# A 96-byte tile at the end of the right side of SBUF in a hybrid pooling, linear-attention and MLP block

## The chip, the cores and the metric

One core of one Trainium2 chip. The metric is the device time of one execution in microseconds (us); smaller is better. A core has TensorE (matmuls, PE in the profile; its weight loads are PEld), VectorE (DVE), ScalarE (ACT), GpSimd (POOL), and SyncE (SP), which here issues the DMA transfers. SBUF, the on-chip memory, has 128 partitions; a tile takes the same bytes in each of them, so an address below is a byte within a partition.

## The reference

One block over 16 meta tokens and 1,024 tokens of width 1,024, all in float32:

```python
h = concat([meta, x])
u = rmsnorm(h, norm_mix)
a, q, k, v, r, lr, ga, gb = split(u @ w_in)          # 512, 256, 256, 512, 512, 16, 1024, 1024 columns
p = (trailing means of a over 2, 4, 8, 16 positions, less a, mixed per group) * pool_scale
y_a = p @ w_pool_out
log_a = log_sigmoid(lr @ w_gate_up + b_gate) / 16
o = gla_chunked(q / 8, k, v, log_a)                  # 4 heads, chunks of 64, a state carried across
y_b = (rmsnorm(o) * silu(r)) @ w_gla_out
h = h + (sigmoid(ga) * y_a + sigmoid(gb) * y_b) @ w_out
h = h + square(relu(rmsnorm(h, norm_ffn) @ w_ff1)) @ w_ff2    # d_ff = 4096
return rmsnorm(h, norm_final)[16:]
```

## The kernel before

**Numbers in two parts.** A float32 operand is split into `hi` (rounded to the type fp32r) and `lo` (the rest): ScalarE copies, VectorE subtracts (in `split`, L607 and L608; in the weight ring, L75 and L76). A product is then three matmuls, hi x hi, hi x lo, lo x hi (`mm3`, L258, L259, L260). In a call `mm3(ps, n, lhs, rhs)` the `lhs` is the stationary operand, which is loaded into TensorE's array, and the `rhs` is the moving one, which streams through it. "Product" below means one accumulated run of four such triples, 12 matmuls, mostly of 128x512.

**Stages, in their order.**
1. `start` (L389): eight row tiles of x are normed and transposed into `th0`/`tl0` (tokens 0 to 511 behind the 16 meta tokens) and `th1`/`tl1` (tokens 512 to 1023). Beside that `v_tile` (L348) multiplies each row tile (stationary) with the two column halves of the v weights, `vw0` (272 columns, with those of lr) and `vw1` (256): nine tiles each, one of them for the meta tokens.
2. Blocks of a and k (`a_block`, `k_block`, through `project`, L265), each as two pieces of 264 columns and one of 512, all streamed from `th`/`tl`, and the pooling.
3. `pairs_of_projections` (L686): q, r, gb and ga, two column blocks at a time with seven products instead of eight (P1 to P7, Strassen's scheme). P1 and P2 stream `th0` behind the meta tokens, P5 and P3 `th1`, P6, P7 and P4 the difference tiles `t0`, `t1`, `t2`. The inner part of the linear attention runs beside it.
4. `gla` (L1105): the state across chunks, with `ya_block` and `yb_block` as filler. `yb_block` (L1002) streams `yg`; its second half of the tokens runs on into the next stage.
5. `out_tile` (L1177): for each of eight row tiles the product with `w_out`, first the columns 0 to 511 from `wo0`, then 512 to 1023 from `wo1`, with `MH`/`ML`, views of `th`/`tl`, as stationary operands. Each is 24 matmuls, two products.
6. `ff1` (L1304): 16 turns (NPAIR) of seven products, in the order P6, P1, P7, P5, P4, P2, P3. P4 streams `t4h`/`t4l`, P6 and P7 `wo0`'s memory, the others `th`/`tl`. The results go to DRAM (`hf_dram`).
7. `ff2` (L1433): seven sums m = 0 to 6 over 16 steps i, each step one product of 12 matmuls (four row tiles times three). Both operands are split into slots that are dealt out in turn (`next_slot`, L598): four in `w1h`/`w1l` and three in `fxh`/`fxl`. Beside m = 0 the blocks of `w_ff2` are loaded.

The order on TensorE is the order of the program text; the other engines' is made by the scheduler from the program. All DMA transfers are issued by SP in one queue.

**Memory.** Two stacks of tiles grow towards each other (`Stack`, L35; L116): `left` from low addresses, `right` from the end of SBUF downwards. A tile is pushed when a stage needs it and popped when a later stage opens. On the right stand, over the run, `xr`, `vw0`, `vw1`, `vo`; then `rawp0`, `rawp1`, `fs`, `s3`, `u2p`, `u3p` and the tiles of the inner linear attention (`n`, `f`, `ends`, `g`, `gi`); then `yg1`, `yg0`, `o`, `gi`, `v`, `sr`, `on`, `kt`, `w`; then `u2p`, `rawx0`, `wo1`; then `fs`, `s3`, `u3p`, `t4h`, `t4l`, `rawx1`; then `bt`, `fxh`, `fxl`. Each has a size per partition that is a multiple of 128 bytes. On the left stand `raw0`, `raw1` (load buffers), `w1h`, `w1l`, `th0`, `tl0`, `th1`, `tl1`, `t0` to `t2`, `wo0`, `acc`, `h`, the four `w2` tiles, `c` and others.

In the kernel before, the right side ends at byte 229,344, which is 1,791 x 128 + 96. As every size there is a multiple of 128, every tile on the right begins 96 bytes past a multiple of 128 (`t4h` at 202,720 = 1,583 x 128 + 96). From `raw0` (23,424 = 183 x 128) on, the working tiles of the left begin at multiples of 128 (`th1` at 81,792 = 639 x 128). Within a tile, rows mostly are multiples of 512 bytes. Two exceptions: a row of `th0` has 528 columns, 2,112 bytes, so its rows begin at 0 and 64 bytes past a multiple of 128 by turns, and the tokens behind the 16 meta tokens begin another 64 bytes on; and a row of `vw0` has 272 columns, 1,088 bytes.

Of the kernel before, what the change touches and what calls it, by code (L numbers as in the profile page):

```python
# [7 lines left out]
F32 = mybir.dt.float32  # L8
# [6 lines left out]
P = 128  # L15
# [88 lines left out]
def kernel(  # L104
# [9 lines left out]

    act, dve, pool, pe = nc.scalar, nc.vector, nc.gpsimd, nc.tensor
    left, right = Stack(tc, "left"), Stack(tc, "right")  # L116

    psp, ps_open = {}, []

# [1375 lines left out]
    banks()  # L1495
    left.pop_to(0)
    right.pop_to(0)


# [33 lines left out]
```

## Time and profile before

| | |
|---|---|
| median of 3 runs | 1259.6 us (1257.75 to 1259.92) |
| the profiled execution | 1261.11 us, span 1259.2 us, mean granted clock of TensorE 0.994 |
| busy in the span | PE 1223.6 us, PEld 998.9, DVE 865.8, ACT 634.6, POOL 74.1 |
| DMA | 192.23 MB, 153 GB/s over the span |

The span runs from the first to the last instruction of the program; the execution's own time lies 1.9 us above it. A busy share is an average over stages with different limits. Matmuls overlap: one of 128x512 is shown with some 390 to 400 ns, and the next one starts 220 to 240 ns behind it. So the pace of TensorE is read from the starts in its timeline, not from the durations. A row of the timeline gives the start, the duration, the engine, the source line, the operation, out<-in by the program's tile names without their last numbers (`th0` and `th1` are both `th`, `wo0` and `wo1` both `wo`; a name that stands for both operands appears once), the shapes, and, where the engine sat idle before, for how long and what ended that.

### The profile page before, as it was taken

The numbers are of one execution on the slowest core, as the hardware profiler recorded it, in microseconds if no ns is written. First come the engines' busy times: TensorE is split into PE (matmuls) and PEld (weight loads), VectorE is DVE, ScalarE is ACT, GpSimd is POOL, SyncE is SP. The second block draws the span as 40 slices with busy tenths as digits, with TensorE's granted clock in tenths as the row PEclk, the third lists the DMA queues.
The fourth block names the chain that finished last, engine by engine and source line by source line (L and its number), as shares of the span: only waits on it lengthen the run. The fifth ranks groups of instructions, "written<-read, shape, count | busy, mean of one in ns | idle before, by whom it ended". The sixth has DMA issues, their size and how long they took to land.

```text
span 1259.2 us, 18413 instructions
## 1 busy us (share of the span) xinstructions
PE 1223.6 (97%) x6807; PEld 998.9 (79%) x6807; DVE 865.8 (69%) x1421; ACT 634.6 (50%) x1119; POOL 74.1 (6%) x95
## 2 busy tenths in 40 slices
PE   8999999999999999999999999999999999999997
PEld 6999877777777777788778888888878788888776
DVE  5635549686787478834896676676664886887685
ACT  6623456676666334523664455454453444445444
POOL 0000052332220000000000000000000000000000
PEclk9999999999999999999999999999999999999999
DMA  8312353334337975931245454444479763332532
GB/s 241 95 39 85 94 133 83 120 101 134 92 128 244 322 248 183 332 117 51 100 134 160 134 167 144 149 152 151 157 251 379 258 203 104 94 96 89 168 92 83
DMA packets 153401, 192.23 MB, mean 153 GB/s; under 512 B 12096, under 2 KB 89168, under 8 KB 153312
## 3 DMA queue, kind: packets, MB, share of 16 engines
q1 hardware_dynamic: 153312, 191.06, 47.3%
q8 instruction: 53, 0.87, 0.3%
q14 instruction: 36, 0.29, 0.1%
HBM read 129.14 MB, written 61.88 MB: 152 GB/s over the span
## 4 chain that ended last, share of the span: by engine, by line
PE 72%; DMA 10%; DVE 9%; ACT 5%; issue 3%; SPq 1%; POOL 0%; DVEq 0%; ACTq 0%; POOLq 0%
PE b_o L259 7%; PE b_o L260 7%; PE b_o L258 7%; PE b_mm L258 6%; PE b_mm L260 6%; PE b_mm L259 5%; PE b_y L258 5%; PE b_y L260 5%; PE b_y L259 5%; PE b_z L258 3%; PE b_z L259 3%; PE b_sc L258 3%; PE b_z L260 3%; PE b_sc L259 3%; PE b_sc L260 3%
## 5 line engine op out<-in xcount | busy, mean ns | idle before, releaser
L607 ACT ACTIVATE w1h<-raw 128x512 fp32r<-128x512 f32 x106 | 66.0, 624 | 57.8 <-PE b_sc L259 19.5
L258 PE MATMUL b_sc<-th,w1h 128*128 128x512 f32 x216 | 86.2, 399 | 2.4 <-ACT u2p L718 1.8
L258 PE MATMUL b_z<-th,w1h 128*128 128x512 f32 x216 | 85.6, 396 | 0.7 <-DVE c L726 0.7
L259 PE MATMUL b_z<-tl,w1h 128*128 128x512 f32 x216 | 85.0, 393 | 0.4 <-DVE tl L1219 0.4
L259 PE MATMUL b_sc<-tl,w1h 128*128 128x512 f32 x216 | 85.1, 394 | 0.0
L260 PE MATMUL b_z<-th,w1l 128*128 128x512 f32 x216 | 84.8, 393 | 0.0
L608 DVE TENSOR_TENSOR w1l<-raw,w1h 128x512 fp32r<-128x512 f32 x106 | 72.8, 687 | 17.1 <-ACT w1h L607 17.1
L260 PE MATMUL b_sc<-th,w1l 128*128 128x512 f32 x216 | 84.4, 391 | 0.0
L607 ACT ACTIVATE w1h<-fs 128x512 fp32r<-128x512 f32 x81 | 50.9, 628 | 54.5 <-PE b_y L259 30.2
L258 PE MATMUL b_o<-w1h 128*128 128x512 f32 x192 | 75.5, 393 | 2.7 <-DVE h L1359 1.7
L259 PE MATMUL b_o<-w1l,w1h 128*128 128x512 f32 x192 | 75.9, 395 | 1.2 <-DVE w1l L608 1.2
L260 PE MATMUL b_o<-w1h,w1l 128*128 128x512 f32 x192 | 76.0, 396 | 0.1
L258 PE MATMUL b_mm<-th,w1h 128*128 128x512 f32 (+1 forms) x208 | 72.3, 348 | 0.9 <-DVE c L734 0.9
L608 DVE TENSOR_TENSOR w1l<-fs,w1h 128x512 fp32r<-128x512 f32 x81 | 56.9, 703 | 23.0 <-ACT w1h L607 22.9
L259 PE MATMUL b_mm<-tl,w1h 128*128 128x512 f32 (+1 forms) x208 | 71.1, 342 | 0.0
L260 PE MATMUL b_mm<-th,w1l 128*128 128x512 f32 (+1 forms) x208 | 71.0, 342 | 0.0
L607 ACT ACTIVATE w1h<-bt 128x512 fp32r<-128x512 f32 x45 | 28.3, 630 | 57.7 <-issue 33.9
L1407 DVE TENSOR_TENSOR bt<-w,w 128x512 f32<-128x512 f32 x80 | 54.7, 683 | 2.3 <-DMA w<-in_w_ff_dram 2.3
L258 PEld LDWEIGHTS b_sc<-th,w1h 128*128 128x128 f32 x216 | 40.5, 188 | 13.7 <-ACT u2p L718 2.2
L259 PE MATMUL b_o<-fxl,fxh 128*128 128x512 f32 x128 | 50.2, 392 | 0.6 <-DVE small L217 0.6
L258 PE MATMUL b_mm<-wo,th 128*128 128x512 f32 x128 | 50.6, 395 | 0.0
L260 PE MATMUL b_o<-fxh,fxl 128*128 128x512 f32 x128 | 50.4, 393 | 0.0
(375 smaller groups left out, 3353.8 us busy)
## 6 DMA issues: line engine op xcount, KB each, us to landing
hf_dram<-h SPq DMA_DIRECT2D x112, 256.0 KB, 2.1
raw<-hf_dram SPq DMA_DIRECT2D x112, 256.0 KB, 2.7
w<-in_w_ff_dram SPq DMA_DIRECT2D x64, 256.0 KB, 4.8
raw<-in_w_in_dram SPq DMA_DIRECT2D x22, 512.0 KB, 4.6
raw<-in_w_ff_dram SPq DMA_DIRECT2D x16, 512.0 KB, 4.4
rawx<-in_w_ff_dram SPq DMA_DIRECT2D x16, 512.0 KB, 4.5
rawp<-in_w_in_dram SPq DMA_DIRECT2D x10, 512.0 KB, 4.9
xs<-in_x_dram SPq DMA_DIRECT2D x8, 512.0 KB, 5.7
```

The source lines that it names most:

```text
L258: pe.matmul(ps, ah, bh, start=first and i == 0, stop=False, skip_group_check=more)
L259: pe.matmul(ps, ah, bl, start=False, stop=False, skip_group_check=more)
L260: pe.matmul(ps, al, bh, start=False, stop=last and i == n - 1, skip_group_check=more)
L607: act.activation(hi, a, ACT.Copy)
L608: dve.tensor_tensor(lo, a, f32(hi), ALU.subtract)
L1407: dve.tensor_tensor(bt, w, S["w2"][q[3:]][:, i], ALU.add if q[2] == "+" else ALU.subtract)
```

## The change

A third stack on the right side gets a single tile, `pad`, of 24 float32 values (96 bytes) in each partition, before anything else is pushed there, and gives it up at the end. No instruction writes or reads it. It lies at bytes 229,248 to 229,343, so every tile on the right begins 96 bytes lower, at a multiple of 128 (229,248 = 1,791 x 128; `t4h` at 202,624 = 1,583 x 128). The tiles on the left stay where they are.

```diff
     left, right = Stack(tc, "left"), Stack(tc, "right")
+    edge = Stack(tc, "right")
+    edge.push("pad", [P, 24], F32)
...
     left.pop_to(0)
     right.pop_to(0)
+    edge.pop_to(0)
```

## The prediction

> **What bounds the kernel now.** I read the page first, its span and the chain of work that ended last.
>
> ```profile
> span 1259.2 us, 18413 instructions
> ...
> PE 72%; DMA 10%; DVE 9%; ACT 5%; issue 3%; SPq 1%; POOL 0%; DVEq 0%; ACTq 0%; POOLq 0%
> ```
>
> TensorE carries 72% of the chain. So a change that makes other engines or transfers quicker is worth little, and one that alters the pace of matmuls is worth what it alters, wherever nothing else is waited for. The change moves the address of every tile on the right side of SBUF and nothing else: no instruction is added, removed or reordered by it. The question is therefore whether TensorE, VectorE, ScalarE or a transfer does the same work at another pace when a tile begins 96 bytes past a multiple of 128 (right side now) instead of on one (left side now, right side after).
>
> The trace of before can answer that, since the same instruction runs on tiles of both sides. I went to the timeline of TensorE, to stretches without idle time, and took the start of the first matmul of each product. A product is four calls of three matmuls, 12 in all, each 128x512, so the distance between two such starts is 12 matmuls. First FF1:
>
> ```profile
> 703.59 0.40 PE L258 MATMUL b_y<-t4h,w1h 128*128 128x512 f32 x1
> ...
> 706.40 0.40 PE L258 MATMUL b_sc<-th,w1h 128*128 128x512 f32 x1
> ...
> 709.16 0.39 PE L258 MATMUL b_z<-th,w1h 128*128 128x512 f32 x1
> ...
> 711.88 0.39 PE L258 MATMUL b_y<-wo,w1h 128*128 128x512 f32 x1
> ...
> 722.76 0.40 PE L258 MATMUL b_y<-t4h,w1h 128*128 128x512 f32 x1
> ```
>
> In "b_y<-t4h,w1h" the first name behind the arrow is the operand that streams through (moving), the second the one that is loaded into the array (stationary). The product from `th1`, a left tile, takes 711.88 - 709.16 = 2.72 us, 226.7 ns a matmul. I call this the floor. The product from `t4h`/`t4l`, the only ones here on the right, takes 706.40 - 703.59 = 2.81, and the one after it, again from a left tile, still 2.76. The whole turn of seven products takes 722.76 - 703.59 = 19.17 where seven floors are 7 x 2.72 = 19.04: 0.13 us too much in every turn, all of it at and just behind the right tile.
>
> Is it the side, or the remainder of the address? The left side has misaligned reads too. In the pairs of projections P1 and P2 stream `th0` from its 17th column on, 64 bytes into rows of 2,112 bytes (16.5 x 128):
>
> ```profile
> 175.36 0.39 PE L258 MATMUL b_y<-t2h,w1h 128*128 128x512 f32 x1
> ...
> 178.08 0.40 PE L258 MATMUL b_sc<-th,w1h 128*128 128x512 f32 x1
> ...
> 180.88 0.40 PE L258 MATMUL b_z<-th,w1h 128*128 128x512 f32 x1
> ```
>
> Both operands of both products are left tiles. The aligned one (`t2h`) takes 2.72, the one at 64 bytes 2.80. So the remainder matters, not the side. FF2 shows it more finely, because its seven operand slots (four of `w1h`/`w1l` on the left, three of `fxh`/`fxl` on the right) are dealt out in turn:
>
> ```profile
> 1000.03 0.40 PE L258 MATMUL b_o<-fxh,w1h 128*128 128x512 f32 x1
> ...
> 1002.84 0.40 PE L258 MATMUL b_o<-fxh 128*128 128x512 f32 x1
> ...
> 1005.59 0.39 PE L258 MATMUL b_o<-w1h 128*128 128x512 f32 x1
> ...
> 1008.35 0.39 PE L258 MATMUL b_o<-w1h 128*128 128x512 f32 x1
> ...
> 1011.08 0.40 PE L258 MATMUL b_o<-fxh 128*128 128x512 f32 x1
> ...
> 1013.84 0.40 PE L258 MATMUL b_o<-w1h,fxh 128*128 128x512 f32 x1
> ...
> 1016.64 0.39 PE L258 MATMUL b_o<-w1h 128*128 128x512 f32 x1
> ...
> 1019.39 0.40 PE L258 MATMUL b_o<-fxh,w1h 128*128 128x512 f32 x1
> ```
>
> One operand from each side costs 2.81 (first product) and 2.80 (sixth), whichever of the two moves; both from the right cost 2.75 and 2.76, both from the left 2.76, 2.73 and 2.75, with the rest of the excess at the changes between them. It looks as if the two reads of TensorE disturb each other when their remainders differ. Whether it is that or the misaligned read alone, after the change both read tiles on multiples of 128, like the floor's. The turn is 1019.39 - 1000.03 = 19.36, against 19.04: 0.32 us too much.
>
> **The change, part by part.** The pad itself holds 96 bytes from start to end and is never written or read. It costs space alone. The sizes of all tiles pushed on the right are multiples of 128 bytes, so all of them move together. Terms:
>
> FF1: 16 turns (NPAIR) of 0.13, 2.1 us. TensorE is what it waits for, so all of it counts.
>
> FF2: 112 products are 16 turns. The first 16 products (m = 0) lie beside their loads:
>
> ```profile
> 935.00:978.00 43.00, 41.31 (x170) 32.82 (x170) 20.59 (x33) 16.60 (x28) 0.00 (x0) 0.96 0.98 357
> 978.00:1165.00 187.00, 186.93 (x812) 152.09 (x812) 147.80 (x247) 81.89 (x147) 0.00 (x0) 1.00 0.45 140
> ```
>
> The columns are the stretch, its length, the busy time of PE, PEld, DVE, ACT and POOL, granted clock, DMA share and GB/s. The DMA engines are 98% busy there, and what they load lies on the left, so I put nothing down for it (bounds 0 and 16/7 x 0.32 = 0.7). In the other 96 products PE never pauses: 96/7 x 0.32 = 4.4 us.
>
> Output projection, second half of the columns (`wo1` on the right; the first half has `wo0` on the left):
>
> ```profile
> 569.81 0.39 PE L258 MATMUL b_mm<-wo,th 128*128 128x512 f32 x1
> ...
> 572.53 0.40 PE L258 MATMUL b_mm<-wo,th 128*128 128x512 f32 x1
> ...
> 575.35 0.39 PE L258 MATMUL b_mm<-wo,th 128*128 128x512 f32 x1
> ```
>
> The last product from `wo0` takes 2.72, the first from `wo1` 2.82. Eight tiles of two halves are 16 products, up to 0.10 each, 1.6; with the 0.08 of the next rows 1.3, and some of it lies beside waits for the norm, so I take 1.2 (bounds 0 and 1.6).
>
> The yb products stream `yg`, on the right:
>
> ```profile
> 498.71 0.48 PE L258 MATMUL b_mm<-yg,w1h 128*128 128x512 f32 x1 [0.78 <-DVE c L1023]
> ...
> 504.40 0.40 PE L258 MATMUL b_mm<-yg,w1h 128*128 128x512 f32 x1
> ...
> 507.20 0.40 PE L258 MATMUL b_mm<-yg,w1h 128*128 128x512 f32 x1
> ...
> 527.91 0.51 PE L258 MATMUL b_mm<-yg,w1h 128*128 128x512 f32 x1 [0.80 <-ACT w1h L75]
> ```
>
> 507.20 - 504.40 = 2.80, 0.08 over the floor; 16 products (four blocks, two halves, two outputs) make 1.3. But this stage pauses for VectorE and for a weight block that ScalarE splits, and those come no sooner when PE is early. I take about half, 0.7 (bounds 0 and 1.3).
>
> The v tiles of the start stream `vw`, on the right, against `th`:
>
> ```profile
> 67.99 0.28 PE L258 MATMUL b_mm<-vw,th 128*128 128x256 f32 x1
> ...
> 70.87 0.28 PE L258 MATMUL b_mm<-vw,th 128*128 128x256 f32 x1
> ...
> 117.30 0.28 PE L258 MATMUL b_mm<-th,w1h 128*128 128x264 f32 x1
> ...
> 120.20 0.29 PE L258 MATMUL b_mm<-th,w1h 128*128 128x264 f32 x1
> ```
>
> Twenty-four matmuls of 256 columns take 2.88; at the floor's pace by column they would take 24 x 256/512 x 0.2267 = 2.72. The 0.16 can go wholly in the four tiles where `vw1` meets the aligned `th1`: 0.64. In the others one side stays at 64 bytes in every other row (`th0`, and `vw0` with rows of 1,088 bytes). What is left there I take from the second pair: 264 columns of `th0`, at 0 and 64 by turns, take 2.90 for 24 against 2.81 by the floor, 0.09. So the four tiles of `vw1` with `th0` gain some 0.07 each, 0.3, and those of `vw0` next to nothing. Together 0.9 (bounds 0, and 18 x 0.16 = 2.9).
>
> Other engines, edits with one answer:
>
> ```profile
> L608 DVE TENSOR_TENSOR w1l<-raw,w1h 128x512 fp32r<-128x512 f32 x106 | 72.8, 687 | 17.1 <-ACT w1h L607 17.1
> L607 ACT ACTIVATE w1h<-raw 128x512 fp32r<-128x512 f32 x106 | 66.0, 624 | 57.8 <-PE b_sc L259 19.5 <-PE b_y L259 17.8 <-issue 6.0
> ...
> L608 DVE TENSOR_TENSOR fxl<-raw,fxh 128x512 fp32r<-128x512 f32 x48 | 32.8, 684 | 0.6 <-ACT fxh L607 0.6
> ...
> L607 ACT ACTIVATE fxh<-raw 128x512 fp32r<-128x512 f32 x48 | 29.8, 620 | 13.3 <-PE b_o L260 6.1 <-DMA raw<-hf_dram 3.4 <-issue 3.1
> ```
>
> The split of a left tile into `w1` (all left) takes 687 and 624 ns, into `fx` (right) 684 and 620. The misaligned side isn't slower, so alignment gives these engines nothing. A load of the same 512 KB to the left and to the right:
>
> ```profile
> raw<-in_w_ff_dram SPq DMA_DIRECT2D x16, 512.0 KB, 4.4
> rawx<-in_w_ff_dram SPq DMA_DIRECT2D x16, 512.0 KB, 4.5
> ```
>
> At most 0.1 us a load, asked for a turn ahead: nothing, and if the cover were gone, the 0.1.
>
> Sum: 2.1 + 4.4 + 1.2 + 0.7 + 0.9 = 9.3 us. The profiled execution took 1261.1, 1.5 above the median of the runs, with a span of 1259.2. I take the gain off both: 1251.8 for a profiled execution, 1259.6 - 9.3 = 1250.3 for the median. What is next late in FF2 is VectorE, 147.80 of 187 us busy: 79%, and 80% at the floor's pace, so it can follow.
>
> **A rule that speaks against it.** The Trainium skill, "SBUF — State Buffer", in its note on SBUF cachelines, makes 16 bytes the unit that a read is charged by. Since 96 is six such lines, by that rule a contiguous read is the same before and after, and the time stays 1259.6. "TensorE: Matmul & The Clock Gate" (Part 2, the fill step) says that throughput is purely the N columns fed in, and gives the two operands independent read ports; by that too nothing changes. The trace disagrees: the same 12 x 512 columns take 2.72 or 2.81, and 64 bytes, four lines, are enough.
>
> **Rivals.** *No effect*, 1259.6: the slow products would stem from something that goes with the right tiles (their distance, the slots), or the pad might be rounded to a size that leaves the remainder. For it: I see remainders only through the tiles that have them. Against it: the slow left product at 178.08. 6%.
>
> *PE gains and waits instead*, at the largest term. If VectorE's bursts at the ends of m in FF2 set the pace, the 4.4 are lost: 9.3 - 4.4 = 4.9, 1254.7. Against it: the 80% above. 10%.
>
> *All of it lands*, also where I put waits: 2.1 + 16 x 0.32 + 1.6 + 1.3 + 2.9 = 13.0, 1246.6. Against it: the loads of m = 0, and the 64-byte rows. 6%.
>
> *Slower*: a quicker PE catches up with its feeders, pauses longer, and the clock drops.
>
> ```profile
> 935.68 0.47 PE L258 MATMUL b_o<-w1h 128*128 128x512 f32 x1 [1.72 <-DVE h L1359]
> ...
> 937.01 0.63 PE L260 MATMUL b_o<-w1h,w1l 128*128 128x512 f32 x1
> ...
> 940.41 0.39 PE L259 MATMUL b_o<-fxl,w1h 128*128 128x512 f32 x1
> ```
>
> Behind a pause of 1.72 us eight matmuls take 940.41 - 937.01 = 3.40 instead of 1.81, 1.6 us lost (0.96 granted in that stretch). Its place would be FF2, where each m ends in a burst on VectorE. It decides from (9.3 + 2.5)/1.6, eight such pauses more; then 1259.6 - 9.3 + 8 x 1.6 = 1263.1. Against it: before has one in FF2, and the denser stretch behind it has clock 1.00. 3%.
>
> **How the numbers follow.** The forecast, gains of 6 to 12 us, has 75%. Faster by over 0.2% (2.5 us, about what a measurement of this kernel tells from no change): 75 + 10 + 6 = 91, less 1 for a part-loss that falls inside 2.5: 90%. Within 0.2%: 6 + 1 = 7%. Slower: 3%. The range goes from 1246.5, all of it landing, to 1255.0, where FF2's term is lost; outside lie no effect, slower, and part of the waits.
>
> **What would show it.** In the timeline, products of `t4h`, `wo` (second half) and `yg` at 2.72; the turn of FF1 at 19.04 and of FF2 at 19.04; P1 of the pairs still 2.80, and 264 columns of `th` still 2.90, since they lie on the left. Splits still some 685 and 622 ns. I am wrong if the FF2 turn stays near 19.36, or if it falls and the span doesn't.

## The result, and the profile after

Six runs of the changed kernel took 1252.2 us in the median (1249.28 to 1255.1), six of the kernel before 1259.19. The ratio is 0.9947, 95% interval 0.9929 to 0.9964: 0.5% faster, 7.0 us, where 9.3 were forecast. A second series gave 1249.99 against 1257.7, ratio 0.995 (0.9931 to 0.9969); one run of the kernel before in it, 1346.9 us at a granted clock of 0.849, is left out as slow. The profiled execution of after took 1249.28 us with a span of 1247.4 and a granted clock of 0.996.

The same lines of the page, after (the three instructions more are semaphore instructions of SyncE and ScalarE, which the prediction had not counted on):

```profile
span 1247.4 us, 18416 instructions
...
PE 76%; DVE 9%; DMA 8%; ACT 4%; issue 3%; SPq 1%; POOL 0%; DVEq 0%; ACTq 0%; POOLq 0%
```

In the timeline of TensorE after (the two added source lines move `mm3` from L258 to L260), the first matmul of each product, in FF1 and then one turn of FF2:

```profile
698.01 0.39 PE L260 MATMUL b_y<-t4h,w1h 128*128 128x512 f32 x1
...
700.73 0.39 PE L260 MATMUL b_sc<-th,w1h 128*128 128x512 f32 x1
...
703.45 0.39 PE L260 MATMUL b_z<-th,w1h 128*128 128x512 f32 x1
...
717.05 0.39 PE L260 MATMUL b_y<-t4h,w1h 128*128 128x512 f32 x1
```

```profile
992.03 0.39 PE L260 MATMUL b_o<-fxh,w1h 128*128 128x512 f32 x1
...
1011.07 0.39 PE L260 MATMUL b_o<-fxh,w1h 128*128 128x512 f32 x1
```

The product of `t4h` takes 2.72 us where it took 2.81, the one behind it 2.72 instead of 2.76, and both turns 19.04 instead of 19.17 and 19.36. These rows are typical: of the 15 products of `t4h` without a pause all take 2.81 before, and after all but the first (2.76) take 2.72. The output projection from `wo1`, the yb products, the v tiles and P1 of the pairs:

```profile
568.11 0.39 PE L260 MATMUL b_mm<-wo,th 128*128 128x512 f32 x1
...
570.83 0.39 PE L260 MATMUL b_mm<-wo,th 128*128 128x512 f32 x1
```

```profile
499.55 0.39 PE L260 MATMUL b_mm<-yg,w1h 128*128 128x512 f32 x1
...
502.27 0.39 PE L260 MATMUL b_mm<-yg,w1h 128*128 128x512 f32 x1
...
512.52 0.50 PE L260 MATMUL b_mm<-yg,w1h 128*128 128x512 f32 x1 [1.14 <-ACT w1h L75]
```

```profile
66.61 0.28 PE L260 MATMUL b_mm<-vw,th 128*128 128x256 f32 x1
...
69.49 0.28 PE L260 MATMUL b_mm<-vw,th 128*128 128x256 f32 x1
```

```profile
178.28 0.40 PE L260 MATMUL b_sc<-th,w1h 128*128 128x512 f32 x1
...
181.08 0.40 PE L260 MATMUL b_z<-th,w1h 128*128 128x512 f32 x1
```

`wo1` went from 2.82 to 2.72 and `yg` from 2.80 to 2.72. P1 stays at 2.80, as forecast: both its operands lie on the left. The v tile does not move: 2.88 before, 2.88 after. The 264-column pieces stay at some 2.90 as well, as forecast.

The two profiles differ by 11.8 us of span, more than the medians do. The starts of the same instructions show where:

| start in the timeline, us | before | after | difference | added since the row above |
|---|---|---|---|---|
| first product of `wo1` | 572.53 | 568.11 | -4.42 | -4.42 |
| a product of `t4h` in FF1 | 703.59 | 698.01 | -5.58 | -1.16 |
| a product of `fxh` in FF2 | 1000.03 | 992.03 | -8.00 | -2.42 |
| end of the span | 1259.2 | 1247.4 | -11.8 | -3.8 |

The last three steps, 7.4 us, lie where the matmuls became quicker. A second profile of the changed kernel, with a span of 1248.0 us, has 7.2 there. The first step is within the scatter: two kernels that are the same as before up to FF1 or FF2 (the pad in FF2 alone, and the kernel before with P4 of FF1 in two pieces, both below) reached their first product of `wo1` at 569.92 and 565.74. So three executions of the same stretch differ by 6.8 us, and none of the 4.42 can be put down to the change.

### The profile page after: what moved, and what is told of

Its sections match the earlier page's. It is cut to its first block, busy times and chain, and to the rows that moved or that the text cites. A ratio compares the mean times of both kernels' runs of the same rounds, so it can differ in the third digit from the quotient of the medians.

```text
span 1247.4 us, 18416 instructions
## 1 busy us (share of the span) xinstructions
PE 1213.6 (97%) x6807; PEld 997.3 (80%) x6807; DVE 866.0 (69%) x1421; ACT 635.3 (51%) x1119; POOL 72.2 (6%) x95
## 4 chain that ended last, share of the span: by engine, by line
PE 76%; DVE 9%; DMA 8%; ACT 4%; issue 3%; SPq 1%; POOL 0%; DVEq 0%; ACTq 0%; POOLq 0%
PE b_o L261 7%; PE b_o L262 7%; PE b_o L260 7%; PE b_mm L262 6%; PE b_mm L260 6%; PE b_mm L261 6%; PE b_y L260 5%; PE b_y L261 5%; PE b_y L262 5%; PE b_sc L260 3%; PE b_sc L261 3%; PE b_z L260 3%; PE b_sc L262 3%; PE b_z L261 3%; PE b_z L262 3%
## 5 line engine op out<-in xcount | busy, mean ns | idle before, releaser
L260 PE MATMUL b_sc<-th,w1h 128*128 128x512 f32 x216 | 86.4, 400 | 2.5 <-ACT u2p L720 1.8
L260 PE MATMUL b_z<-th,w1h 128*128 128x512 f32 x216 | 85.3, 395 | 0.2 <-DVE c L728 0.2
L260 PE MATMUL b_o<-w1h 128*128 128x512 f32 x192 | 75.6, 394 | 2.8 <-DVE h L1361 1.8
L260 PE MATMUL b_mm<-th,w1h 128*128 128x512 f32 (+1 forms) x208 | 72.0, 346 | 0.9 <-DVE c L736 0.9
L260 PEld LDWEIGHTS b_sc<-th,w1h 128*128 128x128 f32 x216 | 40.9, 190 | 13.5 <-ACT u2p L720 2.2
L260 PE MATMUL b_mm<-wo,th 128*128 128x512 f32 x128 | 50.4, 394 | 0.0
```

Of the source, the lines that this page charges most:

```text
L260: pe.matmul(ps, ah, bh, start=first and i == 0, stop=False, skip_group_check=more)
```

## The experiments

**Both sides misaligned alike.** The theory 'pair' of the prediction ("the two reads of TensorE disturb each other when their remainders differ") against 'own' (a read is slow when it is misaligned itself).

```diff
     lrT_meta = left.push("lrT_meta", [16, META], F32)
+    left.push("pad", [P, 24], F32)
...
-    edge = Stack(tc, "right")
-    edge.push("pad", [P, 24], F32)
...
```

> A 96-byte tile is pushed on the left, ahead of the load buffers, and none on the right: the tiles of both sides begin 96 bytes past a multiple of 128. Theory 'pair' (a product is slow when the remainders by 128 of its two operands differ): the products of t4h take 2.72 us and the turn of FF2 19.04 as in the changed kernel, and the time is near the changed kernel's 1252.2. Rival 'own' (a read is slow when its own remainder is not 0): all 512-column products, those of th and w1h too, take some 2.80; some 340 products by 0.08 are 27 us, so about 1286.

1251.02 us, ratio 0.9949 (0.9931 to 0.9967). The timeline:

```profile
719.15 0.39 PE L259 MATMUL b_y<-t4h,w1h 128*128 128x512 f32 x1
...
721.88 0.39 PE L259 MATMUL b_sc<-th,w1h 128*128 128x512 f32 x1
...
724.60 0.39 PE L259 MATMUL b_z<-th,w1h 128*128 128x512 f32 x1
```

```profile
994.34 0.39 PE L259 MATMUL b_o<-fxh,w1h 128*128 128x512 f32 x1
...
1013.38 0.39 PE L259 MATMUL b_o<-fxh,w1h 128*128 128x512 f32 x1
```

2.73, 2.72 and 19.04: none of these tiles begins at a multiple of 128, their products run at the floor, and the time is that of the change. 'Own' falls; what counts is the difference between the two operands.

**Other differences.** The pad of the change with another size:

```diff
-    edge.push("pad", [P, 24], F32)
+    edge.push("pad", [P, 8], F32)      # right side at 64; with 16: at 32
```

> The pad on the right has 32 bytes instead of 96, so the tiles there begin 64 past a multiple of 128. If the unit that counts is 128 bytes: t4h 2.80, the turn of FF2 some 19.3, time about that of the kernel before, 1259. If 64 bytes would do: t4h 2.72, the turn 19.04, about 1252. By P1 of the pairs in the kernel before (2.80 with every other row at 64) I expect the first.

> The pad on the right has 64 bytes, so the tiles there begin 32 past a multiple of 128. If the unit is 128 or 64 bytes: t4h 2.80, the turn of FF2 some 19.3, about 1259. If the unit is 32 bytes, or 16 as the cacheline rule has it: t4h 2.72, the turn 19.04, about 1252.

At 64 the time was 1256.55 us, ratio 0.9984 (0.9966 to 1.0001); at 32 it was 1256.47, 0.9987 (0.9968 to 1.0005): neither can be told from no change. The rows of the first and then of the second:

```profile
705.53 0.40 PE L260 MATMUL b_y<-t4h,w1h 128*128 128x512 f32 x1
...
708.29 0.40 PE L260 MATMUL b_sc<-th,w1h 128*128 128x512 f32 x1
...
711.06 0.39 PE L260 MATMUL b_z<-th,w1h 128*128 128x512 f32 x1
```

```profile
705.11 0.40 PE L260 MATMUL b_y<-t4h,w1h 128*128 128x512 f32 x1
...
707.91 0.40 PE L260 MATMUL b_sc<-th,w1h 128*128 128x512 f32 x1
...
710.67 0.39 PE L260 MATMUL b_z<-th,w1h 128*128 128x512 f32 x1
```

At 64 the product of `t4h` takes 2.76 and the one behind it 2.77 (I had expected 2.80 for the first), at 32 they take 2.80 and 2.76. So neither 16, 32 nor 64 bytes is the unit. That is shown by the paces; the times alone can't tell.

**One term alone.** The pad is pushed when FF2 opens:

```diff
+        right.push("pad", [P, 24], F32)
         S["bt"] = right.push("bt", [P, 2, HALF], F32)
```

> The 96-byte tile is pushed only when FF2 opens, so that bt, fxh and fxl alone are at multiples of 128. If the terms add up as in the prediction: t4h still 2.81, the turn of FF2 19.04, and the time 4.4 to 5 us under the kernel before, about 1254.5. If the gain of FF2 were taken back by waits for VectorE: turn 19.04, but idle time of PE in FF2 up by as much, and about 1259.

1254.34 us against 1258.5, ratio 0.9966 (0.9949 to 0.9982): 4.2 us.

```profile
701.04 0.40 PE L258 MATMUL b_y<-t4h,w1h 128*128 128x512 f32 x1
...
703.85 0.40 PE L258 MATMUL b_sc<-th,w1h 128*128 128x512 f32 x1
...
995.32 0.39 PE L258 MATMUL b_o<-fxh,w1h 128*128 128x512 f32 x1
...
1014.36 0.39 PE L258 MATMUL b_o<-fxh,w1h 128*128 128x512 f32 x1
```

`t4h` still 2.81, the turn of FF2 19.04. The largest term stands by itself, at 4.2 us by the medians (the interval of the ratio makes it 2.3 to 6.4). VectorE takes a little of it back: the longest wait of TensorE late in FF2 grows from 1.24 to 1.38 us, and another from 0.63 to 0.71.

**Is 128 the unit?** The rows of `th0` are made a multiple of 128 long, 17 x 128 bytes, so that P1 is aligned by the rule of the change.

```diff
-    for h, n in ((0, HALF + META), (1, HALF)):
+    for h, n in ((0, HALF + 2 * META), (1, HALF)):
...
-    OFF = (META, 0)
+    OFF = (2 * META, 0)
...
-    WITH_META = [(0, 0, MP), (0, MP, MP), (1, 0, HALF)]
+    WITH_META = [(0, META, MP), (0, META + MP, MP), (1, 0, HALF)]
...
```

> The changed kernel, and the rows of th0 and tl0 get 544 columns instead of 528 (17 x 128 bytes), with the meta tokens at 16 to 31 and the others from 32 on, so that P1 and P2 of the pairs stream aligned rows; wgu moves up the left stack to make the room. Theory 'pair': P1 takes 2.72 us instead of 2.80 and the product behind it 2.72; 22 products (P1 and P2 of 11 pairs) by 0.1 make 2.2 us under the changed kernel. Rival: the stage waits for VectorE, ScalarE and transfers as well (its chain has them), P1 falls to 2.72 and the time doesn't: the same as the changed kernel.

1251.26 us, ratio 0.995 (0.9931 to 0.997), against 1249.99 of the changed kernel in the same series. Its P1:

```profile
177.05 0.40 PE L259 MATMUL b_sc<-th,w1h 128*128 128x512 f32 x1
...
179.82 0.40 PE L259 MATMUL b_z<-th,w1h 128*128 128x512 f32 x1
```

2.77, not 2.72: both theories miss. With 17 x 128 bytes every other row lies 128 bytes off those of `w1h` by remainder of 256, so I suspected that the unit is 256. Then the change would work only because both sides stand at 128 past a multiple of 256 (`t4h` at 202,624 and `th1` at 81,792 both do). Three pads tested it, in each of which every tile begins at a multiple of 128:

```diff
-    edge.push("pad", [P, 24], F32)
+    edge.push("pad", [P, 56], F32)     # with 88, 152: 256 and 512 bytes off
...
```

> The changed kernel with a pad of 224 bytes instead of 96 (wgu moves up the left stack to make the room), so tiles of both sides begin at multiples of 128 but those of the right 128 bytes off those of the left by remainder of 256. If 128 bytes is the unit that counts: t4h 2.72 us and the turn of FF2 19.04. If the unit is 256 or more, as the P1 of the run with rows of 17 x 128 bytes has it (231 ns a matmul, not 226.7): t4h some 2.77, the turn some 19.2 to 19.3.

> The same with a pad of 352 bytes: the right side is 256 bytes off the left by remainder of 512. If the unit is 256 (or 128): t4h 2.72, the turn of FF2 19.04. If it is 512 or more: some 2.75 to 2.80, 19.1 to 19.3.

> The same with a pad of 608 bytes: 512 bytes off by remainder of 1024. Since rows of w1h and fxh are read in steps of 512 bytes within the tiles already at the floor, I expect t4h 2.72 and the turn 19.04, whatever the unit up to 512.

One execution each: 1254.13, 1250.65 and 1250.87 us. No time can be told from one execution (the kernel before goes from 1252.33 to 1263.19 in this series), so the paces decide. The rows of 128 off, then those of 256 off:

```profile
718.46 0.40 PE L259 MATMUL b_y<-t4h,w1h 128*128 128x512 f32 x1
...
721.25 0.39 PE L259 MATMUL b_sc<-th,w1h 128*128 128x512 f32 x1
...
723.98 0.39 PE L259 MATMUL b_z<-th,w1h 128*128 128x512 f32 x1
...
994.02 0.40 PE L259 MATMUL b_o<-fxh,w1h 128*128 128x512 f32 x1
...
1013.30 0.40 PE L259 MATMUL b_o<-fxh,w1h 128*128 128x512 f32 x1
```

```profile
718.70 0.39 PE L259 MATMUL b_y<-t4h,w1h 128*128 128x512 f32 x1
...
721.42 0.39 PE L259 MATMUL b_sc<-th,w1h 128*128 128x512 f32 x1
...
993.35 0.39 PE L259 MATMUL b_o<-fxh,w1h 128*128 128x512 f32 x1
...
1012.39 0.39 PE L259 MATMUL b_o<-fxh,w1h 128*128 128x512 f32 x1
```

With 512 bytes off the two numbers are 2.72 and 19.04 as well. All runs by how far the right side lies off the left, by remainder of 256:

| difference | kernel | product of `t4h`, us | turn of FF2, us |
|---|---|---|---|
| 0 | changed; both at 96; 256 off; 512 off | 2.72 | 19.04 |
| 32 | pad of 64 bytes | 2.80 | 19.32 |
| 64 | pad of 32 bytes | 2.76 | 19.26 |
| 96 | before | 2.81 | 19.36 |
| 128 | pad of 224 bytes | 2.79 | 19.28 |

So 128 is not the unit: at a difference of 128 the turn is nearly as slow as before. Differences that are multiples of 256 are at the floor; 160 to 224 were not tried with a pad, and what in the chip counts in 256 bytes no run shows. Below, rows "agree" where their remainders by 256 are the same.

**The rest of it, P1 and P2 of the pairs.** With 256 as the unit, the rows of `th0` get 9 x 256 bytes:

```diff
-    for h, n in ((0, HALF + META), (1, HALF)):
+    for h, n in ((0, HALF + 4 * META), (1, HALF)):
...
-    OFF = (META, 0)
+    OFF = (4 * META, 0)
...
```

> The changed kernel with rows of 576 columns (9 x 256 bytes) in th0 and tl0, the meta tokens at 48 to 63 and the others from 64 on, so that P1 and P2 of the pairs begin at the same remainder of 256 as w1h (wgu moves up, u2p of FF1 is pushed later, to make the room). If the unit is 256: P1 2.72 instead of 2.80 us; 22 products by up to 0.1 are 2 us under the changed kernel, some 1248, less what the stage waits for anyway. If 512: P1 some 2.75, and no difference in time that can be told.

```profile
176.28 0.39 PE L259 MATMUL b_sc<-th,w1h 128*128 128x512 f32 x1
...
179.00 0.39 PE L259 MATMUL b_z<-th,w1h 128*128 128x512 f32 x1
```

P1 is at the floor, 2.72. The time was 1249.76 us against 1257.8, ratio 0.9938 (0.9914 to 0.9961). That is the lowest ratio of all, but its interval covers those of the changed kernel (0.9947 and 0.995), so a further gain isn't shown.

**Why the v tiles gained nothing.** P4 of FF1 in two pieces, in the changed kernel and in the kernel before:

```diff
-            mm3(b, 4, lambda k: (ah[:, k], al[:, k]), lambda k: (bh[:, k], bl[:, k]), first=not more, more=more)
+            for c in (slice(0, 384), slice(384, HALF)) if p == "P4" else (slice(0, HALF),):
+                mm3(b[:, c], 4, lambda k: (ah[:, k], al[:, k]), lambda k: (bh[:, k, c], bl[:, k, c]), ...)
```

> The changed kernel; P4 of FF1 is done in two pieces of 384 and 128 columns (24 matmuls instead of 12, the same values). The 512-column matmul comes every 226.7 ns and the 256-column one of the v tiles every 120.0, aligned or not: 106.7 for 256 columns and 13.3 for each matmul. Theory 'fixed cost': 384 columns take 173.3 ns and 128 columns 66.7, so P4 takes 12 x 240 = 2.88 us. Rival 'weights': 120 ns is what a weight load allows, so 128 columns take some 120 too, and P4 about 3.5 us.

> The kernel before with the same split of P4, so t4h at 96 past a multiple of 128. If the extra cost of a misaligned pair goes by length, 384 columns come every 173 + 6 = 179 ns or so; if it belongs to matmuls over a certain length, as the v tiles (256 columns, no difference seen) would have it, the 384-column ones show it and the 128-column ones don't; if splitting removes it, P4 takes what it takes in the changed kernel.

One execution each, 1260.61 and 1263.84 us. Of P4, the first and the seventh of the twelve 384-column matmuls and the first two of the 128-column ones, then the first matmul of the next product, in the changed kernel and then in the one before:

```profile
720.67 0.33 PE L260 MATMUL b_y<-t4h,w1h 128*128 128x384 f32 x1
...
721.73 0.33 PE L260 MATMUL b_y<-t4h,w1h 128*128 128x384 f32 x1
...
722.77 0.22 PE L260 MATMUL b_y<-t4h,w1h 128*128 128x128 f32 x1
722.83 0.27 PE L261 MATMUL b_y<-t4l,w1h 128*128 128x128 f32 x1
...
724.06 0.45 PE L260 MATMUL b_sc<-th,w1h 128*128 128x512 f32 x1
```

```profile
718.61 0.34 PE L258 MATMUL b_y<-t4h,w1h 128*128 128x384 f32 x1
...
719.67 0.34 PE L258 MATMUL b_y<-t4h,w1h 128*128 128x384 f32 x1
...
720.73 0.22 PE L258 MATMUL b_y<-t4h,w1h 128*128 128x128 f32 x1
720.79 0.27 PE L259 MATMUL b_y<-t4l,w1h 128*128 128x128 f32 x1
...
722.01 0.45 PE L258 MATMUL b_sc<-th,w1h 128*128 128x512 f32 x1
```

The last six of 384 columns take 722.77 - 721.73 = 1.04 where the rows agree, 173.3 ns each, just what 'fixed cost' gives, and 1.06 where they differ by 96. But the first six take 1.06 in both kernels, and why, no run shows. Over all twelve it is 2.10 against 2.12, under 2 ns a matmul. The 128-column ones take 724.06 - 722.83 = 1.23 and 722.01 - 720.79 = 1.22 for eleven, some 111 ns each in both, not the 66.7 of 'fixed cost'. P4 as a whole takes 3.39 where the rows agree: not its 2.88, and near the 3.5 of the rival. What bounds the 128-column ones I call the weight load, as the rival does, but no run shows that apart. (The Trainium skill, "TensorE: Matmul & The Clock Gate", section on LDWEIGHTS, gives a load as its columns divided by 1.2, in ns, which for 128 columns makes an estimate of 106.7 ns, near the 111 measured.)

The v tiles themselves were run at other differences too, by the pads above. The one that starts at 67.99 in the kernel before and at 66.61 in the changed one, with the right side at 32:

```profile
68.89 0.28 PE L260 MATMUL b_mm<-vw,th 128*128 128x256 f32 x1
...
71.70 0.28 PE L260 MATMUL b_mm<-vw,th 128*128 128x256 f32 x1
```

It takes 2.81 at a difference of 32, and 2.88 at 0 and at 96. So at 256 columns rows that agree aren't the fastest, and 120.0 ns isn't the least that such a matmul can take. The 226.7, 173.3 and 120.0 ns at 512, 384 and 256 columns, all with rows that agree, lie on one line, 13.3 ns and the columns; but the 264-column pieces, whose rows differ, take 2.90 for 24 where that line gives 2.96. So the line is no rule. At a difference of 96 the penalty is some 7 ns at 512 columns (2.80 and 2.81 against 2.72 for twelve), under 2 at 384 and none at 256 and 128; why it goes with the length so, stays open.

## Why the prediction was right, point by point

- **That the pace of matmuls depends on the addresses, and that the pad restores it:** right, for all four tiles with 512 columns (`t4h`, `fxh`, `wo1`, `yg`).
- **FF1, 2.1:** the turn fell from 19.17 to 19.04, 16 x 0.13 = 2.1. From the first matmul of FF1 (623.31 before, 617.98 after) to the first of FF2 (935.68 and 928.41) it is 1.9.
- **FF2, 4.4:** the turn fell by 0.32, and alone this gave 4.2 us by the medians. In the two profiles, from the first matmul of m = 1 (983.33 and 975.38) to the end of the span, it is 3.9. "In the other 96 products PE never pauses" was read from a stretch that ends at 1165; behind it there are two pauses, and the longer one grew. It is the wait for this matmul, before and after:

```profile
1212.69 0.51 PE L259 MATMUL b_o<-w1l,w1h 128*128 128x512 f32 x1 [1.24 <-DVE w1l L608]
```

```profile
1201.56 0.50 PE L261 MATMUL b_o<-w1l,w1h 128*128 128x512 f32 x1 [1.37 <-DVE w1l L610]
```

- **Output projection, 1.2:** from the first product of `wo1` to the first matmul of FF1 it is 50.78 us before and 49.87 after, so 0.9.
- **yb, 0.7:** the pace came, the time can't be seen. Waits in this stretch moved: 1.14 us at 512.52, where the kernel before has none (515.88), and none at 524.38, where it had 0.80 (527.91). From the first yb product to the first of `wo1` it is 93.33 us before and 92.95 after, and 93.74 in the second profile of after.
- **The start, 0.9:** wrong. The step that failed is "at the floor's pace by column they would take 24 x 256/512 x 0.2267 = 2.72". With rows that agree, 24 of 256 columns take 2.88, the same as before; the pace by column of 512 doesn't hold for 256. Without this term the sum is 8.4. What can be seen in the profiles is 1.9 + 3.9 + 0.9 = 6.7, and 7.0 was measured.
- **"It looks as if the two reads of TensorE disturb each other when their remainders differ":** that the difference decides is shown, by both sides at 96; that the two reads disturb each other is an explanation that no run shows apart. And the remainder is one of 256, not of 128 as the change and the prediction had it. Here the prediction had luck: a pad of 224 bytes brings the right side to multiples of 128 as well, and its turn of FF2 is 19.28. My left-side example, P1, would have been slow with rows at multiples of 128 too.
- **Other engines:** as forecast. The splits take 684 and 624 ns for left tiles and 684 and 621 for right ones after, 687 and 624, 684 and 620 before.
- **The rivals:** no effect and slower didn't come, nor did a loss of the whole FF2 term. VectorE did follow (150.55 of 187 us busy from 971 to 1158, the same part of FF2, against 147.80).

The Trainium skill, "TensorE: Matmul & The Clock Gate" (Part 2, step by step), says that loading the next tile's weights takes no read bandwidth from the running matmul, and "SBUF — State Buffer" (note on SBUF cachelines) counts 16-byte lines. By both alone the pad would change nothing. The table by differences shows that it does for these operands, and the measurement decides; whether the weight load takes read bandwidth after all, no run shows.

## What to carry to other kernels

Where matmuls of 512 columns run back to back and load weights for each, compare the starts of equal matmuls on different tiles: a few per cent between them is worth a look at the addresses. What should agree is the remainder by 256 of the rows of the two operands, not the alignment of either, so a row length that isn't a multiple of 256 bytes slows the products as a tile does that begins off. Shorter matmuls are to be measured by themselves: neither the pace nor the penalty of 512 columns carries over to 256.

## What the runs showed of the hardware that was not expected

- The pace of a 512-column matmul with its own weight load: 226.7 ns when the rows of both operands agree by remainder of 256, up to 234 when they differ by 32, 64, 96 or 128. The first products behind a slow one are slow as well (2.76 behind `t4h`).
- The penalty by length, at a difference of 96: some 7 ns at 512 columns, under 2 at 384, none at 256 and 128. At 256 columns rows that differ by 32 are even quicker, 2.81 against 2.88 us for 24.
- 226.7 ns at 512 columns, 173.3 at 384 (in the second half of a product), 120.0 at 256, all with rows that agree, and some 111 at 128, where agreement makes no difference.
